# Convolution and max pool: pooled row pairs with a shared middle-row product, seeded by a PSUM to PSUM copy, with GpSimd preparing the input

## The chip, the cores and the metric

One core of one Trainium2 chip. The time is the device time of one execution in microseconds (us), the median over runs; lower is better. The engines are PE (TensorE: matmuls), ACT (ScalarE), DVE (VectorE), POOL (GpSimd) and SP (SyncE, which here only issues DMAs). Each engine works through its own list of instructions in order, and waits at an instruction until the semaphores that it names have come.

## The reference

A 3x3 convolution with zero padding over 16 images of 64 channels and 64x64 pixels, to 128 channels, and then the maximum over 2x2 pixels:

```python
batch, c_in, h, w, c_out, k = 16, 64, 64, 64, 128, 3
x_pad = np.pad(x, ((0, 0), (0, 0), (1, 1), (1, 1)))
conv[b, co] += weight[co, ci, kh, kw] * x_pad[b, ci, kh:kh+h, kw:kw+w]   # over ci, kh, kw
output[b, c, i, j] = np.max(conv[b, c, 2*i:2*i+2, 2*j:2*j+2])
```

All arrays are float32; the matmuls take bf16 operands.

## The kernel before

Two images are worked on at a time: the 64 channels of the first lie on partitions 0 to 63, those of the second on 64 to 127. A matmul with 64 rows of weights uses one half of PE's rows, so a matmul for the one image (L96, into tile pa) and one for the other (L97, into pb) run side by side; the two together are called a pass here. Weights are loaded, each of the nine taps is copied twice beside itself (L52, L53), transposed by PE (L55) and cast to bf16 by ACT (L57), so that each tap's weights lie on both halves of the partitions.

For each pair of images p (8 of them), the float32 rows come in as two pieces of 1 MB (xraw_t and xraw_b, issued on SP's queue), ACT casts the upper half into xpad (L72) and DVE the lower (L73), and POOL clears the two padding rows (L70, L71). Then come 8 chunks c of 8 rows of convolution. For each chunk PE runs nine passes, one a tap, that add up in the PSUM tiles pa and pb; the moving operand is 8 rows of 64 columns of xpad, shifted by the tap (512 columns, or 8x63 = 504 where the tap looks left or right). ACT copies each PSUM tile to SBUF (L107, 512 columns), DVE takes the maximum over neighbouring columns (L109) and then over neighbouring rows (L113) into oacc, which ACT's queue stores in two pieces a pair (L101 and L122, 16 stores in all).

The order of instructions on each engine is set by a scheduler, from the dependences between tiles. The tile pools allow three chunks in PSUM and two pairs of images in SBUF.

Of the kernel before, what the change touches and what calls it, by code (L numbers as in the profile page):

```python
# [1 line left out]

# [5 lines left out]


@with_exitstack
def kernel(
    ctx: ExitStack,
    tc: tile.TileContext,
    x: bass.AP,
    weight: bass.AP,
    pool_size: bass.AP,
    out: bass.AP,
):
    nc = tc.nc  # L20
# [16 lines left out]
    xraw_pool = ctx.enter_context(tc.tile_pool(name="xraw_pool", bufs=2))
    xpad_pool = ctx.enter_context(tc.tile_pool(name="xpad_pool", bufs=2))
    colmax_pool = ctx.enter_context(tc.tile_pool(name="colmax_pool", bufs=8))
    oacc_pool = ctx.enter_context(tc.tile_pool(name="oacc_pool", bufs=2))  # L40

    ident = const.tile([128, 128], FP32)
    make_identity(nc, ident)
# [2 lines left out]
    nc.sync.dma_start(out=wraw, in_=weight.rearrange("a b c d -> a (b c d)"))  # L46

    wk = []
    for k in range(K * K):
        wdup = const.tile([CO, 2, CI], FP32, name=f"wdup_{k}")  # L50
        src = wraw.rearrange("a (ci k) -> a k ci", k=K * K)[:, k, :]
        nc.vector.tensor_copy(out=wdup[:, 0, :], in_=src)  # L52
        nc.vector.tensor_copy(out=wdup[:, 1, :], in_=src)  # L53
        wp = wpsum.tile([128, 128], FP32, name="wpsum")
        nc.tensor.transpose(wp, wdup.rearrange("a b c -> a (b c)"), ident)  # L55
        wt = const.tile([128, CO], BF16, name=f"wt_{k}")
        nc.scalar.copy(out=wt, in_=wp)  # L57
        wk.append(wt)

    out_v = out.rearrange("b c h w -> c b (h w)")  # L60

    for p in range(B // 2):
# [1 line left out]
        xraw_t = xraw_pool.tile([128, H // 2, W], FP32, name="xraw_t")
        xraw_b = xraw_pool.tile([128, H // 2, W], FP32, name="xraw_b")
        nc.sync.dma_start(out=xraw_t, in_=xv[:, 0 : H // 2])
        nc.sync.dma_start(out=xraw_b, in_=xv[:, H // 2 : H])

        xpad = xpad_pool.tile([128, HP, W], BF16)
        nc.gpsimd.memset(xpad[:, 0, :], 0.0)  # L70
        nc.gpsimd.memset(xpad[:, H + 1, :], 0.0)  # L71
        nc.scalar.copy(out=xpad[:, 1 : 33, :], in_=xraw_t)  # L72
        nc.vector.tensor_copy(out=xpad[:, 33 : H + 1, :], in_=xraw_b)  # L73

        oacc = oacc_pool.tile([128, 2, HO * WO], FP32)

        for c in range(NCHUNK):
            y0 = c * ROWS
            pa = psum.tile([128, ROWS, W], FP32, name="pa")
            pb = psum.tile([128, ROWS, W], FP32, name="pb")  # L80
            korder = [1, 4, 0, 3, 6, 2, 5, 8, 7]
            for i, k in enumerate(korder):
                kh, kw = k // K, k % K
                st = i == 0
                sp = i == K * K - 1
                rows = xpad[:, y0 + kh : y0 + kh + ROWS]
                if kw == 1:
                    mv = rows.rearrange("p a b -> p (a b)")
                    oa, ob = pa, pb
                elif kw == 0:  # L90
                    mv = rows[:, :, 0 : W - 1]
                    oa, ob = pa[:, :, 1:W], pb[:, :, 1:W]
                else:
                    mv = rows[:, :, 1:W]
                    oa, ob = pa[:, :, 0 : W - 1], pb[:, :, 0 : W - 1]
                nc.tensor.matmul(oa, wk[k][0:CI, :], mv[0:CI], start=st, stop=sp)  # L96
                nc.tensor.matmul(ob, wk[k][CI:128, :], mv[CI:128], start=st, stop=sp)  # L97

            for half, pt in ((0, pa), (1, pb)):
                if half == 0 and c == 5:  # L100
                    nc.scalar.dma_start(  # L101
                        out=out_v[:, 2 * p : 2 * p + 2, 0 : HO * WO // 2],
                        in_=oacc[:, :, 0 : HO * WO // 2],
                    )
                pv = pt
                sb = colmax_pool.tile([128, ROWS, W], FP32, name=f"sb{half}")
                nc.scalar.copy(out=sb, in_=pv)  # L107
                cm = colmax_pool.tile([128, ROWS, WO], FP32, name=f"cm{half}")
                nc.vector.tensor_tensor(  # L109
                    out=cm, in0=sb[:, :, 0::2], in1=sb[:, :, 1::2],  # L110
                    op=mybir.AluOpType.max,
                )
                nc.vector.tensor_tensor(  # L113
                    out=oacc.rearrange("p b (h w) -> p b h w", h=HO)[
                        :, half, y0 // 2 : y0 // 2 + ROWS // 2, :
                    ],
                    in0=cm[:, 0::2, :],
                    in1=cm[:, 1::2, :],
                    op=mybir.AluOpType.max,
                )  # L120

        nc.scalar.dma_start(  # L122
            out=out_v[:, 2 * p : 2 * p + 2, HO * WO // 2 :],
            in_=oacc[:, :, HO * WO // 2 :],
        )


# [33 lines left out]
```

## Time and profile before

| | |
|---|---|
| median of 3 runs | 146.75 us (146.67 to 147.31) |
| span of the profiled execution, first to last instruction | 145.9 us |
| mean granted TensorE clock over the span | 0.995 |
| PE busy | 131.7 us (90%), 1161 matmuls, 1152 of them tap passes' halves |
| DVE busy | 95.2 us (65%) |
| ACT busy | 86.2 us (59%) |
| POOL busy | 8.6 us (6%) |
| DMA | 25.64 MB, mean 176 GB/s |

The page gives no time of its own for the profiled execution beside its span; the runs' median lies 0.85 us above it. Rows of instruction groups read: line, engine, operation, output tile <- input tiles, shape, count | busy us in total, mean ns of one | us that the engine sat idle ahead of it, and what ended the idle time. Rows of a timeline begin with the start and the duration in us. "PEld" is PE's loading of weights, which overlaps its matmuls.

### The profile page before, as it was taken

The page shows a single profiled execution, that of the slowest core. Times are in us where ns is not written, and L with a number is a line of the kernel's source. Part 1 is how long each engine was busy: PE and PEld are TensorE (multiplying, and loading weights), DVE is VectorE, ACT ScalarE, POOL GpSimd, SP SyncE. Part 2 cuts the span into 40 slices and gives each one's busy share as a digit, 9 for nine tenths or more (in the row PEclk, how much of TensorE's full clock was granted, in tenths as well). Part 3 has the DMA queues.
Part 4 walks back from the last instruction along what each step waited for, and adds up shares of the span by engine and source line. Part 5 has one row for each costly group of instructions (what it writes and reads, how often), then busy time and mean ns, then how long its engine had stood idle before and what let it go on. Part 6 is the DMA issues. An engine that isn't in the chain of part 4 may idle for free.

```text
span 145.9 us, 3022 instructions
## 1 busy us (share of the span) xinstructions
PE 131.7 (90%) x1161; PEld 58.0 (40%) x1161; DVE 95.2 (65%) x282; ACT 86.2 (59%) x146; POOL 8.6 (6%) x22
## 2 busy tenths in 40 slices
PE   0159999999999999999999999999999999999930
PEld 0023344444444444444444444444444444444410
DVE  0630287686768685878679676867686858586770
ACT  3174644578555955597367755695559555463640
POOL 2000000030001200030003000300002000000000
PEclk9999999999999999999999999999999999999997
DMA  5999995308960598139840994030302112030303
GB/s 164 409 427 427 395 332 231 144 2 236 384 247 3 133 344 334 57 63 284 369 152 16 259 408 184 7 146 0 144 4 84 60 67 81 13 131 4 144 0 144
DMA packets 6813, 25.64 MB, mean 176 GB/s; under 512 B 528, under 2 KB 528, under 8 KB 4752
## 3 DMA queue, kind: packets, MB, share of 16 engines
q1 hardware_dynamic: 2448, 17.07, 32.3%
q10 hardware_dynamic: 4352, 8.39, 15.1%
q8 instruction: 9, 0.15, 0.4%
q14 instruction: 4, 0.03, 0.1%
HBM read 17.07 MB, written 8.39 MB: 175 GB/s over the span
## 4 chain that ended last, share of the span: by engine, by line
PE 90%; DMA 4%; ACT 2%; DVE 1%; SPq 0%; issue 0%; ACTq 0%
PE pa L96 86%; DMA xraw_t<-in_x_dram 4%; PE pb L97 2%; PE wpsum L55 2%; ACT xpad L72 1%; DVE cm L109 1%; ACT sb L107 0%; DVE oacc L113 0%; SPq L46 0%; ACT wt L57 0%; ACTq L107 0%
## 5 line engine op out<-in xcount | busy, mean ns | idle before, releaser
L96 PE MATMUL pa<-xpad,wt 64*128 64x504 bf16 (+1 forms) x576 | 127.6, 382 | 0.0
L97 PE MATMUL pb<-xpad,wt 64*128 64x504 bf16 (+1 forms) x576 | 127.6, 382 | 0.0
L96 PEld LDWEIGHTS <-wt 64*128 64x128 bf16 x576 | 54.8, 95 | 70.5 <-issue 3.6
L109 DVE TENSOR_TENSOR cm<-sb 128x256 f32<-128x256 f32 x128 | 53.6, 423 | 35.9 <-ACT sb L107 35.9
L107 ACT COPY sb<-pa 128x512 f32<-128x512 f32 x64 | 37.5, 585 | 46.2 <-PE pb L97 33.0
L97 PEld LDWEIGHTS <-wt 64*128 64x128 bf16 x576 | 54.8, 95 | 0.5 <-issue 0.5
L113 DVE TENSOR_TENSOR oacc<-cm 128x128 f32<-128x128 f32 x128 | 36.8, 292 | 3.9
L107 ACT COPY sb<-pb 128x512 f32<-128x512 f32 x64 | 37.9, 592 | 0.0
L72 ACT CAST xpad<-xraw_t 128x2048 bf16<-128x2048 f32 x8 | 15.3, 1909 | 4.9 <-DMA xraw_t<-in_x_dram 4.9
L70 POOL MEMSET xpad<- 128x64 bf16 x8 | 7.5, 937 | 101.2 <-DVE oacc L113 101.2
L73 DVE CAST xpad<-xraw_b 128x2048 bf16<-128x2048 f32 x8 | 9.8, 1226 | 3.4 <-DMA xraw_b<-in_x_dram 3.4
L55 PE MATMUL wpsum<-ident,wdup 128*128 128x128 f32 x9 | 3.5, 452 | 8.3 <-ACT wt L57 4.2
L71 POOL MEMSET xpad<- 128x64 bf16 x8 | 7.3, 918 | 0.0
L55 PEld LDWEIGHTS wpsum<-ident,wdup 128*128 128x128 f32 x9 | 1.6, 187 | 10.4 <-ACT wt L57 6.2
L52 DVE COPY wdup<-wraw 128x64 f32<-128x64 f32 x9 | 1.9, 209 | 3.7 <-DMA wraw<-in_weight_dram 3.7
L57 ACT CAST wt<-wpsum 128x128 bf16<-128x128 f32 x9 | 2.2, 265 | 3.1 <-PE wpsum L55 3.1
L53 DVE COPY wdup<-wraw 128x64 f32<-128x64 f32 x9 | 1.9, 208 | 0.0
L72 ACT ACT_TABLE_LOAD x1 | 1.3, 1283 | 0.7 <-PEq L142 0.7
masks.py:199 POOL TENSOR_SCALAR_AFFINE_SELECT ident<-ident 128x128 f32<-128x128 f32 x1 | 0.3, 292 | 0.0
masks.py:197 POOL MEMSET ident<- 128x128 f32 x1 | 0.2, 204 | 0.3 <-POOLq L142 0.3
L142 POOL MEMSET const-float32-0.0<- 128x1 f32 x1 | 0.1, 98 | 0.2 <-issue 0.2
L142 POOL MEMSET const-bfloat16-1.0<- 128x1 bf16 x1 | 0.1, 101 | 0.0
(2 smaller groups left out, 0.2 us busy)
## 6 DMA issues: line engine op xcount, KB each, us to landing
xraw_t<-in_x_dram SPq DMA_DIRECT2D x8, 1024.0 KB, 8.5
xraw_b<-in_x_dram SPq DMA_DIRECT2D x8, 1024.0 KB, 7.0
out_dram<-oacc ACTq DMA_DIRECT2D x16, 512.0 KB, 3.1
wraw<-in_weight_dram SPq DMA_DIRECT2D x1, 288.0 KB, 2.9
```

Source lines behind the costliest of these rows:

```text
L52: nc.vector.tensor_copy(out=wdup[:, 0, :], in_=src)
L55: nc.tensor.transpose(wp, wdup.rearrange("a b c -> a (b c)"), ident)
L57: nc.scalar.copy(out=wt, in_=wp)
L70: nc.gpsimd.memset(xpad[:, 0, :], 0.0)
L71: nc.gpsimd.memset(xpad[:, H + 1, :], 0.0)
L72: nc.scalar.copy(out=xpad[:, 1 : 33, :], in_=xraw_t)
L73: nc.vector.tensor_copy(out=xpad[:, 33 : H + 1, :], in_=xraw_b)
L96: nc.tensor.matmul(oa, wk[k][0:CI, :], mv[0:CI], start=st, stop=sp)
L97: nc.tensor.matmul(ob, wk[k][CI:128, :], mv[CI:128], start=st, stop=sp)
L107: nc.scalar.copy(out=sb, in_=pv)
L109: nc.vector.tensor_tensor(out=cm, in0=sb[:, :, 0::2], in1=sb[:, :, 1::2], op=mybir.AluOpType.max,)
L113: nc.vector.tensor_tensor(out=oacc.rearrange("p b (h w) -> p b h w", h=HO)[:, half, y0 // 2 : y0 // 2 + ROWS // 2, :], in0=cm[:, 0::2, :], ...
```

## The change

A pooled row is the maximum of two neighbouring rows of the convolution, an even one y0 and the odd one below it, y1. Write x(a) to x(d) for the four input rows that a pair reads, and w0, w1, w2 for the three rows of taps. Then y0 = w0·x(a) + w1·x(b) + w2·x(c) and y1 = w0·x(b) + w1·x(c) + w2·x(d). The change writes both over a common product with the sum of the middle rows, s = x(b) + x(c): y0 = w1·s + (w2 − w1)·x(c) + w0·x(a), and y1 = w1·s + (w0 − w1)·x(b) + w2·x(d). With three columns of taps that is 3 passes for w1·s, 6 for the rest of y0 and 6 for the rest of y1: 15 passes for 8 row pairs, where two chunks took 18.

A group g is now two images and 8 row pairs (16 rows), 32 groups in all. By function:

- load: float32 rows of a group, 0.5 MB a piece, on SP's queue, eight groups ahead (10 buffers).
- do_s (L152) and do_x (L158), on POOL: the row sums s in bf16 from an add of 128x512, and the cast of the rows to bf16, 128x1024. They are written three groups ahead in the program.
- do_c: 3 passes of w1·s into the PSUM tile y0. seed (L180), on ACT: one copy of 128x1024 from y0 to y1, PSUM to PSUM.
- do_a: the 6 other passes into y0. evac (L187), on ACT: y0 to SBUF, in two copies of 128x512.
- do_b: the 6 other passes into y1, on top of the copied product.
- rowmax (L192), on DVE: the maximum of y1 (PSUM) and the copied y0 (SBUF), 2 x 128x512. finish (L200), on DVE: the maximum over neighbouring columns, 512 results from SBUF. Its store (L203) goes on SP's queue, 0.25 MB a group.

y0 and y1 have two PSUM tiles each, taken in turn. Padding rows are left out rather than cleared: the first and last group of an image pair run three passes with 7 rows for 8. At the start, eight matmuls on zeros run ahead of the weights; the weights are cast and subtracted by DVE, ACT and POOL (L86 to L91), transposed in bf16 by PE in 15 steps (L97) and copied out in two pieces (L105 on DVE, L107 on ACT). The order on every engine is the order of the program, with the automatic scheduling switched off.

```diff
+    ctx.enter_context(tc.manual_schedule())
...
+    for i in range(8):
+        yt = y1[(i // 2) % 2]
+        nc.tensor.matmul(
+            yt[:, i % 2], zeros[:, 0:128], zeros, start=True, stop=True, skip_group_check=True
+        )
...
+    nc.gpsimd.tensor_sub(out=wq[:, 7:10, :], in0=wv[:, 6:9, :], in1=wv[:, 3:6, :])
+    nc.gpsimd.tensor_sub(out=wq[:, 10:13, :], in0=wv[:, 0:3, :], in1=wv[:, 3:6, :])
...
-        nc.gpsimd.memset(xpad[:, 0, :], 0.0)
-        nc.gpsimd.memset(xpad[:, H + 1, :], 0.0)
-        nc.scalar.copy(out=xpad[:, 1 : 33, :], in_=xraw_t)
-        nc.vector.tensor_copy(out=xpad[:, 33 : H + 1, :], in_=xraw_b)
...
+        nc.gpsimd.tensor_add(
+            out=ss[p][:, q * R : (q + 1) * R, :], in0=v[:, 0::2, :], in1=v[:, 1::2, :]
+        )
...
+        nc.gpsimd.tensor_copy(out=xb[p][:, 2 * R * q : 2 * R * (q + 1), :], in_=xf[g])
...
+    def do_a(g):
+        p, q = divmod(g, NQ)
+        taps(y0[g % 2], D2, xrows(p, 2 * q * R + 1))
+        taps(y0[g % 2], G0, xrows(p, 2 * q * R - 1), skip=0 if q == 0 else None)
...
+    def seed(g):
+        nc.scalar.copy(out=y1[g % 2], in_=y0[g % 2])
...
+        nc.scalar.copy(out=ev[g][:, half], in_=y0[g % 2][:, half])
...
+        nc.vector.tensor_tensor(
+            out=rm[g][:, half], in0=y1[g % 2][:, half], in1=ev[g][:, half], op=MAX
+        )
...
+        nc.vector.tensor_tensor(
+            out=o, in0=r[:, :, :, 0::2], in1=r[:, :, :, 1::2], op=MAX
+        )
...
+    for g in range(3):
+        do_s(g)
+        do_x(g)
+    do_c(0)
+    seed(0)
+    for g in range(G):
+        if g + LEAD < G:
+            load(g + LEAD)
+        do_a(g)
+        evac(g, 0)
+        if g + 1 < G:
+            do_c(g + 1)
+            seed(g + 1)
+        do_b(g)
+        evac(g, 1)
+        rowmax(g, 0)
+        rowmax(g, 1)
+        finish(g)
+        if g + 3 < G:
+            do_s(g + 3)
+            do_x(g + 3)
```

The order on the engines, at three places. PE before, at the border of two chunks; a chunk's first matmuls wait until ACT has copied the tiles of three chunks earlier (a matmul and the weights that it takes stand in two rows):

```order
L96 LDWEIGHTS wt_7_137
L96 MATMUL pa_216<-xpad_150,wt_7_137 128x512
L97 LDWEIGHTS wt_7_137
L97 MATMUL pb_217<-xpad_150,wt_7_137 128x512
L96 LDWEIGHTS wt_1_95
L96 MATMUL pa_246<-xpad_150,wt_1_95 128x512 [waits Activation_49]
L97 LDWEIGHTS wt_1_95
L97 MATMUL pb_247<-xpad_150,wt_1_95 128x512 [waits Activation_49]
```

PE after, where B(1), into the second y1 tile, ends and A(2), into the first y0 tile, begins:

```order
L128 LDWEIGHTS wt_125
L128 MATMUL y1_1_84<-xb_143,wt_125 128x8x63
L128 LDWEIGHTS wt_125
L128 MATMUL y0_0_81<-xb_143,wt_125 128x512 [waits Activation_49]
L128 LDWEIGHTS wt_125
L128 MATMUL y0_0_81<-xb_143,wt_125 128x512
```

The wait on ACT now is for the copy seed(2), whose source C(2) was written just ahead of B(1). ACT before, over some chunks of the first pair, has only copies out of PSUM, each waiting for its own chunk:

```order
L72 CAST xpad_402<-xraw_t_398 128x2048 [waits DMAHW3_49]
L107 COPY sb0_176<-pa_156 128x512 [waits PE_49]
L107 COPY sb1_181<-pb_157 128x512 [waits PE_49]
L107 COPY sb0_206<-pa_186 128x512 [waits PE_49]
L107 COPY sb1_211<-pb_187 128x512 [waits PE_49]
L107 COPY sb0_236<-pa_216 128x512 [waits PE_49]
```

ACT after, over groups 1 and 2:

```order
L187 COPY ev_216<-y0_1_82 128x512 [waits PE_49]
L180 COPY y1_0_83<-y0_0_81 128x1024 [waits DVE_49,PE_49]
L187 COPY ev_216<-y0_1_82 128x512
L187 COPY ev_262<-y0_0_81 128x512 [waits PE_49]
L180 COPY y1_1_84<-y0_1_82 128x1024 [waits DVE_49,PE_49]
L187 COPY ev_262<-y0_0_81 128x512
```

The copy from y0 to y1 stands between the two copies of a group, and waits for DVE as well, which must have read the y1 tile two groups earlier. POOL before, at the first pairs of images, has two clearings a pair:

```order
masks.py:199 AFFINE_SELECT ident_76<-ident_76 128x128 [waits Pool_49]
L70 MEMSET xpad_402 128x64
L71 MEMSET xpad_402 128x64
L70 MEMSET xpad_654 128x64 [waits PE_49,DVE_49,Activation_49,Pool_49]
L71 MEMSET xpad_654 128x64
```

POOL after, from the fourth pair of images on, waits for a load at each group, and at each new pair for PE, whose use of the tiles s and xb three pairs earlier must have ended:

```order
L152 TENSOR_TENSOR s_423<-xf_292 128x512 [waits DMAHW7_49]
L158 CAST xb_422<-xf_292 128x1024
L152 TENSOR_TENSOR s_601<-xf_336 128x512 [waits DMAHW1_49,PE_49,Pool_49]
L158 CAST xb_600<-xf_336 128x1024 [waits PE_49,Pool_49]
L152 TENSOR_TENSOR s_601<-xf_380 128x512 [waits DMAHW3_49]
```

What was 16 instructions over the main loop is now 64, two a group.

More of the change, by code (lines that the diff above doesn't have):

```diff
@@ L37 @@
[L37 to L43, printed above, removed]
+    NP = B // 2
+    NQ = 4
+    R = HO // NQ
+    G = NP * NQ
+    LEAD = 8
+    const = ctx.enter_context(tc.tile_pool(name="const", bufs=1))
@@ L45 @@
+    ctx.enter_context(tc.manual_schedule())
+    y0 = [psum.tile([128, 2, R, W], FP32, name=f"y0_{i}") for i in range(2)]
+    y1 = [psum.tile([128, 2, R, W], FP32, name=f"y1_{i}") for i in range(2)]
     wraw = const.tile([CO, CI * K * K], FP32)
     nc.sync.dma_start(out=wraw, in_=weight.rearrange("a b c d -> a (b c d)"))
[L48 to L58, printed above, removed]
@@ L60 @@
-    out_v = out.rearrange("b c h w -> c b (h w)")
-    for p in range(B // 2):
-        xv = x[2 * p : 2 * p + 2].rearrange("b c h w -> (b c) h w")
[L64 to L111, printed above, removed]
-                )
[L113 to L124, printed above, removed]
-        )
@@ new lines, with load @@
+    xb, ss, xf = {}, {}, {}
+    def load(g):
+        p, q = divmod(g, NQ)
+        xv = x[2 * p : 2 * p + 2].rearrange("b c h w -> (b c) h w")
+        xf[g] = xf_pool.tile([128, 2 * R, W], FP32, name="xf")
+        nc.sync.dma_start(out=xf[g], in_=xv[:, 2 * R * q : 2 * R * (q + 1), :])
+    for g in range(LEAD):
+        load(g)
+    zeros = const.tile([128, 512], BF16)
+    nc.vector.memset(zeros, 0.0)
+    ident = const.tile([128, 128], BF16)
+    make_identity(nc, ident)
+    for i in range(8):
[3 more added lines that the diff above has]
+        )
@@ new lines @@
+    wv = wraw.rearrange("a (ci k) -> a k ci", k=K * K)
+    wq = const.tile([CO, 16, CI], BF16)
+    nc.vector.tensor_copy(out=wq[:, 1:4, :], in_=wv[:, 3:6, :])
+    nc.vector.tensor_copy(out=wq[:, 4:7, :], in_=wv[:, 0:3, :])
+    nc.scalar.copy(out=wq[:, 0, :], in_=wv[:, 8, :])
+    nc.scalar.copy(out=wq[:, 13:16, :], in_=wv[:, 6:9, :])
+    nc.gpsimd.tensor_sub(out=wq[:, 7:10, :], in0=wv[:, 6:9, :], in1=wv[:, 3:6, :])
+    nc.gpsimd.tensor_sub(out=wq[:, 10:13, :], in0=wv[:, 0:3, :], in1=wv[:, 3:6, :])
@@ new lines @@
+    wt = const.tile([128, 15, CO], BF16)
+    for h, (lo, hi) in enumerate(((0, 8), (8, 15))):
+        tp = y0[1][:, h].rearrange("p a b -> p (a b)").bitcast(BF16)
+        for j in range(lo, hi):
+            nc.tensor.transpose(
+                tp[:, (j - lo) * 128 : (j - lo + 1) * 128],
+                wq[:, j : j + 2, :].rearrange("a b c -> a (b c)"),
+                ident,
+            )
+        src = tp[:, 0 : (hi - lo) * 128]
+        dst = wt[:, lo:hi, :].rearrange("p a b -> p (a b)")
+        if h == 0:
+            nc.vector.tensor_copy(out=dst, in_=src)
+        else:
+            nc.scalar.copy(out=dst, in_=src)
@@ new lines, in wtop, with wbot, taps @@
+    def wtop(m):
+        return wt[0:CI, (m + 1) % 15, :]
+    def wbot(m):
+        return wt[CI:128, m, :]
+    G1, G0, D2, D0, G2 = 0, 3, 6, 9, 12
+    def taps(dst, m0, rows, start=False, skip=None):
+        for kw in (1, 0, 2):
+            i0, i1 = 0, R
+            if skip == 0:
+                i0 = 1
+            if skip == R - 1:
+                i1 = R - 1
+            o0, o1, c0, c1 = (0, W, 0, W) if kw == 1 else (1, W, 0, W - 1) if kw == 0 else (0, W - 1, 1, W)
+            for half, wsel in ((0, wtop), (1, wbot)):
+                lo = half * CI
+                nc.tensor.matmul(
+                    dst[:, half, i0:i1, o0:o1],
+                    wsel(m0 + kw),
+                    rows(lo, i0, i1, c0, c1),
+                    start=start and kw == 1,
+                    stop=True,
+                    skip_group_check=True,
+                )
@@ new lines, in xrows, with get, do_s @@
+    def xrows(p, first):
+        v = xb[p]
+        def get(lo, i0, i1, c0, c1):
+            a = first + 2 * i0
+            return v[lo : lo + CI, a : first + 2 * (i1 - 1) + 1 : 2, c0:c1]
+        return get
+    def do_s(g):
+        p, q = divmod(g, NQ)
+        if q == 0:
+            xb[p] = xb_pool.tile([128, H, W], BF16, name="xb")
+            ss[p] = s_pool.tile([128, HO, W], BF16, name="s")
+        v = xf[g]
+        nc.gpsimd.tensor_add(
+            out=ss[p][:, q * R : (q + 1) * R, :], in0=v[:, 0::2, :], in1=v[:, 1::2, :]
+        )
@@ new lines, in do_b, with evac, rowmax @@
+    def do_b(g):
+        p, q = divmod(g, NQ)
+        taps(y1[g % 2], D0, xrows(p, 2 * q * R))
+        taps(y1[g % 2], G2, xrows(p, 2 * q * R + 2), skip=R - 1 if q == NQ - 1 else None)
+    def seed(g):
+        nc.scalar.copy(out=y1[g % 2], in_=y0[g % 2])
+    ev, rm = {}, {}
+    def evac(g, half):
+        if half == 0:
+            ev[g] = ev_pool.tile([128, 2, R, W], FP32, name="ev")
+        nc.scalar.copy(out=ev[g][:, half], in_=y0[g % 2][:, half])
+    def rowmax(g, half):
+        if half == 0:
+            rm[g] = rm_pool.tile([128, 2, R, W], FP32, name="rm")
+        nc.vector.tensor_tensor(
+            out=rm[g][:, half], in0=y1[g % 2][:, half], in1=ev[g][:, half], op=MAX
+        )
@@ new lines, in finish @@
+    def finish(g):
+        p, q = divmod(g, NQ)
+        o = o_pool.tile([128, 2, R, WO], FP32, name="o")
+        r = rm[g]
+        nc.vector.tensor_tensor(
+            out=o, in0=r[:, :, :, 0::2], in1=r[:, :, :, 1::2], op=MAX
+        )
+        nc.sync.dma_start(
+            out=out[2 * p : 2 * p + 2, :, q * R : (q + 1) * R, :].rearrange(
+                "b c h w -> c b (h w)"
+            ),
+            in_=o.rearrange("p b h w -> p b (h w)"),
+        )
+        del rm[g], ev[g]
+    for g in range(3):
+        do_s(g)
+        do_x(g)
```

26 lines of the change are left out of this document (19 added, 7 removed).

## The prediction

> **What bounds the kernel now.** I read the engine totals first, then the chain of work that ended last, then the groups of instructions by form, then the timeline at the two ends and at the places that the change touches. The totals and the chain's shares by line:
>
> ```profile
> PE 131.7 (90%) x1161; PEld 58.0 (40%) x1161; DVE 95.2 (65%) x282; ACT 86.2 (59%) x146; POOL 8.6 (6%) x22
> ...
> PE pa L96 86%; DMA xraw_t<-in_x_dram 4%; PE pb L97 2%; PE wpsum L55 2%; ACT xpad L72 1%; DVE cm L109 1%; ACT sb L107 0%; DVE oacc L113 0%; SPq L46 0%; ACT wt L57 0%; ACTq L107 0%
> ```
>
> PE is 90% busy and nearly the whole chain is its tap passes; a pass is one L96 and one L97 matmul that run side by side on the two halves of the rows. Nothing but fewer or faster passes, a shorter start or a shorter tail can help. The groups (mean ns of one after the comma):
>
> ```profile
> L96 PE MATMUL pa<-xpad,wt 64*128 64x504 bf16 x384 | 94.9, 381 | 0.0
> L109 DVE TENSOR_TENSOR cm<-sb 128x256 f32<-128x256 f32 x128 | 53.6, 423 | 35.9 <-ACT sb L107 35.9
> L96 PE MATMUL pa<-xpad,wt 64*128 64x512 bf16 x192 | 53.2, 383 | 0.0
> L107 ACT COPY sb<-pb 128x512 f32<-128x512 f32 x64 | 37.9, 592 | 0.0
> L113 DVE TENSOR_TENSOR oacc<-cm 128x128 f32<-128x128 f32 x128 | 36.8, 292 | 3.9
> L72 ACT CAST xpad<-xraw_t 128x2048 bf16<-128x2048 f32 x8 | 15.3, 1909 | 4.9 <-DMA xraw_t<-in_x_dram 4.9
> L55 PE MATMUL wpsum<-ident,wdup 128*128 128x128 f32 x9 | 3.5, 452 | 8.3 <-ACT wt L57 4.2
> L52 DVE COPY wdup<-wraw 128x64 f32<-128x64 f32 x9 | 1.9, 209 | 3.7 <-DMA wraw<-in_weight_dram 3.7
> ```
>
> A matmul's own duration (381 ns) overlaps its successor, so the price of a pass is read from start to start, at the end of the run:
>
> ```profile
> 137.69 0.38 PE L96 MATMUL pa<-xpad,wt 64*128 64x512 bf16 x1
> ...
> 137.90 0.38 PE L96 MATMUL pa<-xpad,wt 64*128 64x512 bf16 x1
> ...
> 138.15 0.58 ACT L107 COPY sb<-pa 128x512 f32<-128x512 f32 x1 [0.87 <-PE pb L97]
> ...
> 138.63 0.59 ACT L107 COPY sb<-pb 128x512 f32<-128x512 f32 x1
> ...
> 139.63 0.38 PE L96 MATMUL pa<-xpad,wt 64*128 64x512 bf16 x1
> 140.10 0.58 ACT L107 COPY sb<-pa 128x512 f32<-128x512 f32 x1 [0.87 <-PE pb L97]
> ...
> 140.72 0.43 DVE L109 TENSOR_TENSOR cm<-sb 128x256 f32<-128x256 f32 x1 [0.53 <-ACT sb L107]
> 141.18 0.29 DVE L113 TENSOR_TENSOR oacc<-cm 128x128 f32<-128x128 f32 x1
> ...
> 142.16 0.38 ACTq L122 DMA_DIRECT2D out_dram<-oacc  x1
> ```
>
> 137.69 and 139.63 are the last passes of two neighbouring chunks: nine passes in 1.94 us, 0.2156 us each. The pass of 137.69 gives way at 137.90 and ScalarE starts on its result at 138.15: 0.25 us from PE to ScalarE. The start:
>
> ```profile
> 3.68 0.22 DVE L52 COPY wdup<-wraw 128x64 f32<-128x64 f32 x1 [3.68 <-DMA wraw<-in_weight_dram]
> ...
> 6.89 1.90 ACT L72 CAST xpad<-xraw_t 128x2048 bf16<-128x2048 f32 x1 [4.88 <-DMA xraw_t<-in_x_dram]
> ...
> 9.37 1.23 DVE L73 CAST xpad<-xraw_b 128x2048 bf16<-128x2048 f32 x1 [3.35 <-DMA xraw_b<-in_x_dram]
> ...
> 11.82 0.27 ACT L57 CAST wt<-wpsum 128x128 bf16<-128x128 f32 x1 [0.68 <-PE wpsum L55]
> 12.25 0.18 PEld L55 LDWEIGHTS wpsum<-ident,wdup 128*128 128x128 f32 x1 [0.44 <-ACT wt L57]
> ...
> 13.60 0.60 PE L96 MATMUL pa<-xpad,wt 64*128 64x504 bf16 x1
> ...
> 14.00 0.63 PE L96 MATMUL pa<-xpad,wt 64*128 64x504 bf16 x1
> ...
> 14.43 0.63 PE L96 MATMUL pa<-xpad,wt 64*128 64x504 bf16 x1
> ```
>
> Weights land at 3.68, 1 MB of images at 6.89, the next at 9.37 (so 0.5 MB takes 1.24 us). Weights then ping-pong between PE and ScalarE; three passes are done by 13.60, when the unbroken run begins. Its first passes are 0.43 us apart; in the chain the pace turns between these rows:
>
> ```profile
> 18.05 0.29 PE pa L96
> 18.55 0.21 PE pa L96
> ```
>
> From ScalarE back to PE: 11.82 + 0.27 = 12.09, and PE resumes at 12.25, 0.16 us.
>
> **The change, part by part.** The sum is made on the span, 145.9 us; the median of the runs shown is 146.75, so 0.85 us lie around the span and stay.
>
> *Passes.* 32 groups (two images, 16 rows) with 15 passes each, 480 for 576: 96 × 0.2156 = 20.7 us less. The eight first groups leave out one row of eight in three passes: 3 passes, 0.65 us less (the eight last groups' saving falls where PE waits for ScalarE anyway, see below). Twelve of the 15 read every second row; the 64x504 form, broken into rows as well, costs 381 ns against 383, so I add nothing; bound: a tenth of 384 passes, 8 us.
>
> *The PSUM to PSUM copy.* PE runs A(g), 6 passes; C(g+1), 3; B(g), 6; A(g+1). A(g+1) adds into the bank that seed(g+1) copies from, so it waits for it. Between C's end and A(g+1) lie B's six passes, 1.29 us. The seed has 1024 columns: 0.59 + 512 × (1.909 − 0.59)/1536 = 1.03 us. Bounds: twice the start-to-start of the L107 copies (138.15 to 138.63), 0.96; twice their duration, 1.18. With the two hand-overs the wait takes 0.25 + 1.03 + 0.16 = 1.44 us, 0.15 more than B covers. Times 31: +4.5 us (+2.5 to +9.2; nothing, if writes to PSUM are much shorter: no row shows one from ScalarE). Ahead of the seed, evac(g,0) starts 0.25 after A and takes 0.59, and C lasts 0.65: it is out of the way. ScalarE's load is 2 × 0.59 + 1.03 = 2.21 us of a group's 3.38 (3.23 of passes and the wait).
>
> *VectorE.* Two maxima of 512 columns with one side in PSUM, and one of 512 from SBUF. By L113 and L109, (0.423 − 0.292)/128 = 1.02 ns a column: 0.69 us each, 2.06 a group. From PSUM no row shows it; below, the 0.59 of ScalarE's copy, above, twice 0.69. Even 1.38 × 2 + 0.69 = 3.45 only touches the group's 3.38. seed(g+2) needs both maxima of g; they end 0.25 + 1.4 us after B(g), and that seed starts a whole A and C (1.94) plus 0.15 after it: hidden, by 0.4.
>
> *GpSimd.* It had 8.6 us of work; now each group needs an add of 512 columns and a cast of 1024. Its rows, with VectorE's beside the two odd ones:
>
> ```profile
> 0.27 0.10 POOL L142 MEMSET const-float32-1.0<- 128x1 f32 x1
> ...
> 0.73 0.20 POOL masks.py:197 MEMSET ident<- 128x128 f32 x1 [0.29 <-POOLq L142]
> ...
> 0.87 0.15 POOL L70 MEMSET xpad<- 128x64 bf16 x1
> ...
> 1.13 0.29 POOL masks.py:199 TENSOR_SCALAR_AFFINE_SELECT ident<-ident 128x128 f32<-128x128 f32 x1
> ...
> 31.34 1.20 POOL L70 MEMSET xpad<- 128x64 bf16 x1 [29.74 <-DVE oacc L113]
> 31.42 1.17 POOL L71 MEMSET xpad<- 128x64 bf16 x1
> ...
> 31.22 1.23 DVE L73 CAST xpad<-xraw_b 128x2048 bf16<-128x2048 f32 x1
> ```
>
> A memset's slope is (0.20 − 0.10)/127 = 0.8 ns a column, the select's (it reads, compares, writes) 1.5. Cast: 0.10 + 1024 × 0.8 = 0.92 to 1.64; it compares nothing, so I take 1.1. Add: one stream at 0.8, 0.51, to two reads at 1.5, 1.64; I take 1.2. Sum 2.3 us a group (1.43 to 3.28). The 0.15 us memset took 1.20 us while VectorE's cast ran and ended with it (32.54 against 32.45): the two shut each other out. If the SBUF maximum does that once a group, GpSimd needs 2.3 + 0.69 = 2.99 of 3.38, still hidden; the margin is 0.39 us.
>
> The Trainium skill, "GPSIMD Engine Reference", section 3.1, measures 4497 ns for a two-input add of 2048 columns, by which (an estimate) the add is about 1.1 us; its section 4.1 calls one-input work roughly line-rate but elementwise work the wrong use of this engine. With those the sum would stay as it is, and no run here shows either figure yet.
>
> *Loads and stores.* Loads go in 32 pieces of 0.5 MB (1.24 us each of 3.38); stores move from ScalarE's queue to SP's, where load(g+9) stands behind the store of g, which waits for VectorE. That load is used eight groups later (27 us), so it hides.
>
> *Start.* GpSimd's two subtractions and the other engines' casts end by 4.9 us; 15 transposes at about 0.1 (bounds 0.05 and the 0.45 of L55's fp32 ones) in two lots with VectorE's copy of 1024 columns (0.16 + 1.04) and ScalarE's 896 (0.92) between give wt by 8.6; the row sum has its 0.5 MB at 5.65 and is ready at 6.9. C(0) at 7.4 takes 1.28 at the slow pace, seed(0) ends near 10.0 and the unbroken run starts at 10.1, again with three passes done: 3.5 us less than 13.60 (4.6 less to 2.0 more). The slow pace of the first eleven passes I leave as it was; if the eight zero matmuls end it, 2.3 us less.
>
> *Tail.* From the last pass's end (139.84) to the store's issue (142.16) it was 2.32; now 0.25 + 3 × 0.69 + 0.05. The last store carries half the bytes: 0.5 us less (up to 1.4 more by the PSUM bound).
>
> Sum: 145.9 − 20.7 − 0.65 + 4.5 − 3.5 − 0.5 = 125.05, and 0.85 around it: **125.9 us**.
>
> **The rivals.** (1) *The seed hides*: if it takes under 0.88 us, PE never waits, 125.9 − 4.5 = 121.4. For it: only 0.15 us decides. Against: the nearest rows give 0.96 at the least. The Trainium skill, "ScalarE: Activation LUTs", section "Step-by-step: what each stage is for", says ScalarE is closer to PSUM and writes there sooner; no run here shows by how much.
>
> (2) *GpSimd becomes the bound.* Its first add starts at 5.65; then 32 groups of p; then B(30), A(31), B(31), 3.9; tail 5.5 and 0.85: 15.9 + 32p. It decides from p = 3.38 on. With the select's rate for the cast, 1.64 + 1.2 + 0.69 = 3.53, 128.9; with both upper ends 3.28 + 0.69 = 3.97, 142.9. A middle one, 3.7, 134.3. For it: the select is the only row that reads, and it is slow. Against: a cast needs less per column.
>
> (3) *Slower: every maximum shuts GpSimd out*, not only the one with both inputs in SBUF; the other two also read one input there. Then p = 2.3 + 3 × 0.69 = 4.37 and the time 155.7. It ends over the old time from p = 4.09. For it: the memset pair above, against one-input work. Against: that cast ran at 0.6 ns a column, faster than any maximum, so it may hold more of the path than they do. The Trainium skill, "SBUF — State Buffer", section "Who interferes with whom", has it that VectorE blocks GpSimd's reads with two SBUF inputs or in its faster two-port modes, not with one; by that rule only L200's maximum counts, as in the sum.
>
> (4) *The passes don't get cheaper*: reading every second row would have to cost 0.054 us a pass (20.9/384) to eat the gain. The two equal forms speak against it.
>
> **How the numbers follow.** Forecast 0.57 (122.5 to 131 by its own bounds), rival 1 0.10, rival 2 0.22, rival 3 0.09, rival 4 0.02. The range 119 to 141 leaves out rival 3, rival 4 and the top of rival 2 (p over 3.91, 0.05), and 0.01 below. Half a per cent is about what can be told from no change here. Faster: 0.57 + 0.10 + 0.22 less 0.02 for p near or over 4.09 = 0.87; within: 0.02; slower: 0.11.
>
> **What the profile after would show.** PE at 480 passes, 0.2156 apart within A, C and B; before each A a gap of about 0.15 us that ScalarE's L180 ends, L180 near 1.03 us; L152 plus L158 near 2.3 us of GpSimd and GpSimd ahead of PE by several groups; L192 and L200 near 0.69; PE's unbroken run from about 10 us. The prediction is wrong if PE's waits end on GpSimd's L152 or L158 in the middle of the run, or if L180's gap is above 0.3 or absent.

## The result and the profile after

The changed kernel takes 120.19 us in the median of five runs (118.44 to 121.77) against 147.17 before: 0.810 of the time, 95% interval 0.804 to 0.816. On another chip it took 119.18 (118.14 to 120.30 in six runs), 0.808 (0.805 to 0.812). A run over 1.5% above the fastest of its kernel counts as slow: it is in the medians and ranges given here but not in the intervals, and where too few others are left no interval is given. The forecast was 125.9 in a range of 119 to 141: the direction and the sum's largest term held, the time came out 5.7 us lower, near the lower end of the range. The profiled execution took 120.19, its span is 118.4. Totals, and the chain's shares by line, of the page after:

```profile
PE 109.7 (93%) x983; PEld 49.9 (42%) x983; DVE 74.8 (63%) x100; ACT 69.7 (59%) x100; POOL 81.8 (69%) x72
...
PE y L128 88%; DMA xf<-in_x_dram 4%; POOL s L152 1%; ACT y L180 1%; DVE rm L192 1%; DVE o L200 1%; SPq L59 0%; DVEq L192 0%
```

PE is still the bound and the chain is its tap passes. GpSimd has gone from 6% to 69% without getting into the chain, but for its first row sum. The chain in order of time (start, us, what):

```profile
5.95 1.27 POOL s L152
...
7.27 0.84 PE y L128 x6
...
8.13 1.01 ACT y L180
...
9.18 103.93 PE y L128 x944
...
114.53 0.69 DVE o L200
```

C(0) waits for the first row sum, A(0) for the first seed, and from 9.18 us on the chain runs through PE alone for 103.93 us. In all of the middle no seed, no row sum and no cast stands in it. The groups that answer to those shown before:

```profile
L192 DVE TENSOR_TENSOR rm<-y,ev 128x512 f32<-128x512 f32 x64 | 41.2, 686 | 34.9 <-PE y L128 33.3
L187 ACT COPY ev<-y 128x512 f32<-128x512 f32 x64 | 37.6, 589 | 37.3 <-PE y L128 37.3
L152 POOL TENSOR_TENSOR s<-xf 128x512 bf16<-128x512 f32 x32 | 45.0, 1408 | 11.3 <-DMA xf<-in_x_dram 9.9
L158 POOL CAST xb<-xf 128x1024 bf16<-128x1024 f32 x32 | 36.8, 1150 | 0.0
L180 ACT COPY y<-y 128x1024 f32<-128x1024 f32 x32 | 31.9, 997 | 1.0 <-PE y L128 0.7
L200 DVE TENSOR_TENSOR o<-rm 128x512 f32<-128x512 f32 x32 | 31.7, 989 | 1.1
```

Two groups in the middle of the run, from the timeline (PE's rows are merged by operand; 6 matmuls are 3 passes), and, last, a row of the list of waits (engine, line waited for: us in total, times, longest us):

```profile
60.28 0.81 PE L128 MATMUL y<-s,wt 64*128 64x512 bf16 x6
...
60.93 2.65 PE L128 MATMUL y<-xb,wt 64*128 64x512 bf16 x24
...
61.13 1.00 ACT L180 COPY y<-y 128x1024 f32<-128x1024 f32 x1
...
62.18 5.00 PEld L128 LDWEIGHTS <-wt 64*128 64x128 bf16 x50 [0.32 <-ACT y L180]
62.35 1.03 POOL L158 CAST xb<-xf 128x1024 bf16<-128x1024 f32 x1
62.42 1.29 DVE L192 TENSOR_TENSOR rm<-y,ev 128x512 f32<-128x512 f32 x2 [1.15 <-PE y L128]
63.41 0.81 PE L128 MATMUL y<-s,wt 64*128 64x512 bf16 x6
63.42 1.27 POOL L152 TENSOR_TENSOR s<-xf 128x512 bf16<-128x512 f32 x1
...
63.75 1.49 DVE L200 TENSOR_TENSOR o<-rm 128x512 f32<-128x512 f32 x1
64.06 2.76 PE L128 MATMUL y<-xb,wt 64*128 64x512 bf16 x24
64.27 1.00 ACT L180 COPY y<-y 128x1024 f32<-128x1024 f32 x1
64.64 1.50 POOL L158 CAST xb<-xf 128x1024 bf16<-128x1024 f32 x1
...
66.66 0.81 PE L128 MATMUL y<-s,wt 64*128 64x512 bf16 x6
...
PEld L128 <- ACT y L180: 3.8, 8, 1.6
```

In the second group C ends at 64.06, the seed runs from 64.27 to 65.27, and B's six passes (1.29) last until 65.35: A begins then, and PE doesn't wait. The first group is a border of two image pairs, where three passes of B leave out a row and B takes 1.21 (1.29 less 3/8 of a pass): it is over at 62.14, the seed at 62.13, and A's weights load at 62.18, with the seed as what they waited for. PE stands for some 0.04 us there. The row of waits has eight such cases, the first seed and the seven borders; in the other 24 groups the seed is hidden, by some 0.04 us. The rows of 63.42 to 64.64 show VectorE and GpSimd holding each other up: L200 begins in the middle of L152 and takes 1.49 us for its usual 0.69, and L158, next to start, takes 1.50 for its usual 1.03. The L158 of 62.35, beside which L192 alone runs, takes its 1.03.

### The profile page after: what moved, and what is told of

It reads as the page before. It is cut to its first block, busy times and chain, and to the rows that moved or that the text cites. A ratio compares the mean times of both kernels' runs of the same rounds, so it can differ in the third digit from the quotient of the medians.

```text
span 118.4 us, 2534 instructions
## 1 busy us (share of the span) xinstructions
PE 109.7 (93%) x983; PEld 49.9 (42%) x983; DVE 74.8 (63%) x100; ACT 69.7 (59%) x100; POOL 81.8 (69%) x72
## 4 chain that ended last, share of the span: by engine, by line
PE 88%; DMA 4%; DVE 1%; POOL 1%; ACT 1%; issue 1%; SPq 0%; DVEq 0%
PE y L128 88%; DMA xf<-in_x_dram 4%; POOL s L152 1%; ACT y L180 1%; DVE rm L192 1%; DVE o L200 1%; SPq L59 0%; DVEq L192 0%
## 5 line engine op out<-in xcount | busy, mean ns | idle before, releaser
L128 PE MATMUL y<-xb,wt 64*128 64x504 bf16 (+3 forms) x768 | 88.5, 377 | 1.1 <-ACT y L180 1.1
L128 PEld LDWEIGHTS <-wt 64*128 64x128 bf16 x960 | 47.5, 95 | 58.4 <-ACT y L180 3.8
L192 DVE TENSOR_TENSOR rm<-y,ev 128x512 f32<-128x512 f32 x64 | 41.2, 686 | 34.9 <-PE y L128 33.3
L187 ACT COPY ev<-y 128x512 f32<-128x512 f32 x64 | 37.6, 589 | 37.3 <-PE y L128 37.3
L152 POOL TENSOR_TENSOR s<-xf 128x512 bf16<-128x512 f32 x32 | 45.0, 1408 | 11.3 <-DMA xf<-in_x_dram 9.9
L158 POOL CAST xb<-xf 128x1024 bf16<-128x1024 f32 x32 | 36.8, 1150 | 0.0
L180 ACT COPY y<-y 128x1024 f32<-128x1024 f32 x32 | 31.9, 997 | 1.0 <-PE y L128 0.7
L200 DVE TENSOR_TENSOR o<-rm 128x512 f32<-128x512 f32 x32 | 31.7, 989 | 1.1
L128 PE MATMUL y<-s,wt 64*128 64x504 bf16 (+1 forms) x192 | 26.4, 382 | 0.3 <-POOL s L152 0.3
L80 PE MATMUL y<-zeros 128*128 128x512 bf16 x8 | 3.6, 630 | 1.2 <-DVE zeros L74 1.2
L107 ACT COPY wt<-y 128x896 bf16<-128x896 bf16 x1 | 0.9, 905 | 2.5 <-PE y L97 2.5
L97 PE MATMUL y<-ident,wq 128*128 128x128 bf16 x15 | 1.6, 269 | 0.8 <-DVE wt L105 0.8
L86 DVE CAST wq<-wraw 128x192 bf16<-128x192 f32 x1 | 0.5, 498 | 2.6 <-DMA wraw<-in_weight_dram 2.6
L97 PEld LDWEIGHTS <-wq 128*128 128x128 bf16 x15 | 1.4, 126 | 1.5 <-issue 0.9
L105 DVE COPY wt<-y 128x1024 bf16<-128x1024 bf16 x1 | 0.7, 692 | 1.0 <-PE y L97 1.0
L91 POOL TENSOR_TENSOR wq<-wraw 128x192 bf16<-128x192 f32 x1 | 0.8, 793 | 0.0
```

What stands on the lines that cost most here:

```text
L80: nc.tensor.matmul(yt[:, i % 2], zeros[:, 0:128], zeros, start=True, stop=True, skip_group_check=True)
L97: nc.tensor.transpose(tp[:, (j - lo) * 128 : (j - lo + 1) * 128], wq[:, j : j + 2, :].rearrange("a b c -> a (b c)"), ident,)
L107: nc.scalar.copy(out=dst, in_=src)
L128: nc.tensor.matmul(dst[:, half, i0:i1, o0:o1], wsel(m0 + kw), rows(lo, i0, i1, c0, c1), start=start and kw == 1, stop=True, skip_group_che ...
L152: nc.gpsimd.tensor_add(out=ss[p][:, q * R : (q + 1) * R, :], in0=v[:, 0::2, :], in1=v[:, 1::2, :])
L158: nc.gpsimd.tensor_copy(out=xb[p][:, 2 * R * q : 2 * R * (q + 1), :], in_=xf[g])
```

## The experiments

**What the shared product is worth: 18 passes.** No row sum, no seed; C takes w1·x(b), A takes w2·x(c) in place of the difference's product, and B begins with w1·x(c):

```diff
-        nc.gpsimd.tensor_add(
-            out=ss[p][:, q * R : (q + 1) * R, :], in0=v[:, 0::2, :], in1=v[:, 1::2, :]
-        )
...
-            lambda lo, i0, i1, c0, c1: st[lo : lo + CI, q * R + i0 : q * R + i1, c0:c1],
+            xrows(p, 2 * q * R),
...
-        taps(y0[g % 2], D2, xrows(p, 2 * q * R + 1))
+        taps(y0[g % 2], G2, xrows(p, 2 * q * R + 1))
...
-        taps(y1[g % 2], D0, xrows(p, 2 * q * R))
+        taps(y1[g % 2], G1, xrows(p, 2 * q * R + 1), start=True)
+        taps(y1[g % 2], G0, xrows(p, 2 * q * R))
...
-        nc.scalar.copy(out=y1[g % 2], in_=y0[g % 2])
```

> The pair isn't shared here: 18 passes a group as in the kernel before, no row sum on GpSimd, no seed copy; the start, the loads, the casts on GpSimd and the tail are as in the changed kernel. Theory (the time went with the passes): PE stays the bound, 96 passes of 0.2156 us come back, 120.2 + 20.7 = 141 us, with GpSimd at about 1.0 us a group. Rival (the gain comes from the start, the casts taken off ScalarE and VectorE and the finer groups): the time stays within 3 us of 120.

138.11 us (137.97 to 139.65), 0.944 of before (0.938 to 0.950). Its chain has one piece of PE:

```profile
7.32 124.90 PE y L128 x1152
```

It begins at 7.32, for there is no first row sum or seed to wait for, and holds 576 passes of 0.217 us. The theory holds: of the whole change's 27.7 us (146.91 to 119.18 on the one chip), this kernel brings 8.4 without the sharing (146.49 to 138.11 on the other), which leaves 19.3 for it. The 96 passes are 20.7; the wait for the first row sum and seed gives about 1.0 of them back (8.96 with three passes done, in the chain of the changed kernel's second run, against 7.32 with none). The 8.4 us lie between two kernels with the same number of passes: 5.9 of them are the unbroken run's earlier start (13.60 with two passes done to 7.32 with none) and 1.3 the rows left out at the borders, both worked out and not taken apart by a run.

**How far the seed hides: its place.** Both copies of y0 go ahead of the next seed in ScalarE's order.

```diff
         evac(g, 0)
+        evac(g, 1)
         if g + 1 < G:
             do_c(g + 1)
             seed(g + 1)
         do_b(g)
-        evac(g, 1)
```

> Only ScalarE's order is changed: both copies of y0 to SBUF go ahead of the next group's seed, which so starts about 1.16 us after A ends and not 0.85. Theory (the seed is hidden, but by less than 0.1 us: in the trace it ends 62.13 and A begins 62.22): PE now waits some 0.27 us before each A, L180 is what ends these waits, and the time is 120.2 + 31 x 0.27 = 128.6 us. Rival (the seed has slack, its wait was priced too high because ScalarE to PE or the copy itself is much shorter): no change, 120.

130.62 us in the median of four runs (128.15 to 130.92), where 128.6 was expected. From the timeline:

```profile
51.43 0.83 PE L128 MATMUL y<-s,wt 64*128 64x512 bf16 x6
51.65 1.07 ACT L187 COPY ev<-y 128x512 f32<-128x512 f32 x2 [1.56 <-PE y L128]
52.08 1.40 PE L128 MATMUL y<-xb,wt 64*128 64x512 bf16 x12
52.61 1.03 ACT L180 COPY y<-y 128x1024 f32<-128x1024 f32 x1
53.70 1.39 PE L128 MATMUL y<-xb,wt 64*128 64x512 bf16 x12 [0.22 <-ACT y L180]
...
54.92 0.81 PE L128 MATMUL y<-s,wt 64*128 64x512 bf16 x6
```

The seed starts 0.53 us behind C's end (52.08) in place of 0.20, ends at 53.64, and A starts 0.06 later. B's passes were over at 53.37: PE stood for 0.33 us, which over 31 groups makes 10.2. The theory holds, and the rows give the price of the way back to PE, 0.06.

**How far the seed hides: its length.** On the kernel with ten more filling matmuls (below), the seed is issued as two copies.

```diff
-        nc.scalar.copy(out=y1[g % 2], in_=y0[g % 2])
+        for half in range(2):
+            nc.scalar.copy(out=y1[g % 2][:, half], in_=y0[g % 2][:, half])
```

> The kernel with the ten filling matmuls (118.4 to 119.3), with the seed as two copies of 512 columns for one of 1024. By the rows of such copies that takes 0.48 + 0.59 = 1.07 us for 0.997. Theory (from PE to ScalarE 0.20, the seed 0.997 and back 0.06 make 1.26 of B's 1.29 us: a margin of 0.03 to 0.09): the longer seed makes PE wait 0.00 to 0.04 us a group, 0 to 1.3 us more, and L180's rows show up as what ends PE's idle time. Rival (the margin is larger, 0.1 us or more): no wait anywhere, 119.0.

123.80 us (123.51 to 124.41), 0.841 of before (0.838 to 0.845): 4.7 us more than with one copy (119.09, on another chip), where 0 to 1.3 was expected.

```profile
61.24 0.83 PE L137 MATMUL y<-s,wt 64*128 64x512 bf16 x6
...
61.89 2.84 PE L137 MATMUL y<-xb,wt 64*128 64x512 bf16 x24
62.11 1.17 ACT L190 COPY y<-y 128x512 f32<-128x512 f32 x2
...
64.56 0.81 PE L137 MATMUL y<-s,wt 64*128 64x512 bf16 x6
```

The two copies take 1.17 us together and not 1.07: two of L187's in a row, which go to SBUF, overlap (1.07 for 2 × 0.59 in the rows of the last run), these two don't. 0.22 + 1.17 + 0.06 is 1.45 us, 0.16 over B's 1.29, and 31 × 0.16 = 5.0. So the miss is the copy's price; the mechanism is the expected one, and it shows how thin the cover is: 0.20 + 0.997 + 0.06 = 1.26 of 1.29.

**More cover for the seed.** C moves between A's two halves (do_a keeps the passes of w2 − w1, do_a2 takes those of w0), and the seed ahead of both copies of y0.

```diff
         taps(y0[g % 2], D2, xrows(p, 2 * q * R + 1))
+
+    def do_a2(g):
+        p, q = divmod(g, NQ)
         taps(y0[g % 2], G0, xrows(p, 2 * q * R - 1), skip=0 if q == 0 else None)
...
         do_a(g)
-        evac(g, 0)
         if g + 1 < G:
             do_c(g + 1)
             seed(g + 1)
+        do_a2(g)
+        evac(g, 0)
+        evac(g, 1)
         do_b(g)
-        evac(g, 1)
```

> PE runs A's first three passes, C of the next group, A's last three passes, B; ScalarE runs the seed and then both copies of y0. The seed now has nine passes (1.94 us) to hide behind and not six (1.29). Theory (the seed is hidden by 0.05 to 0.1 us, so that some executions wait at it and others don't): the trace with no wait gains nothing, but the spread of 118.4 to 121.8 shrinks towards its lower end, median 118 to 119. Rival (the seed has slack and the spread comes from the start): median and spread as in the unedited kernel.

120.53 us (118.39 to 121.71 in six runs), 0.811 (0.806 to 0.816), beside the unedited kernel on the same chip:

> The changed kernel itself, unedited, beside the next three on one chip. Both theories: 118.4 to 122 us as in its first five runs; what is looked for is the spread, and how the span stands to the granted clock.

119.18 (118.14 to 120.30). Neither the median nor the spread shrinks, so the theory on the spread falls: thin as the seed's cover is, it isn't what parts a run of 118.4 from one of 120 or 121. The rival, the start, stays.

**Keeping PE busy ahead of the unbroken run.** awake(n, ys) issues n more matmuls on zeros into the tiles ys.

```diff
         if h == 0:
             nc.vector.tensor_copy(out=dst, in_=src)
+            awake(4, y1)
         else:
             nc.scalar.copy(out=dst, in_=src)
+            awake(2, y1)
...
     do_c(0)
+    awake(4, [y1[1]])
     seed(0)
```

> Ten more matmuls on zeros keep PE busy between the transposes' two lots, behind them, and behind C(0) while ScalarE copies the first seed. The first nine passes behind the first seed took 3.45 us where 1.94 would do, with a granted clock of 0.50 to 0.59. Theory (the idle stretches ahead of them bring the slow pace): the slow stretch goes, 1.5 us less, 118.7. Rival (the pace comes back only after so much time in any case, or the filling matmuls delay C(0)): the same time, or up to 1 us more.

119.09 us (118.44 to 119.27 in five runs), 0.810 (0.808 to 0.813). The same stretch, 9.10 to 11.50 us, in the run of the unedited kernel and in this one (columns: length, PE busy and count, PEld, DVE, ACT, POOL, granted clock, DMA share, GB/s):

```profile
9.10:11.50 2.40, 2.40 (x14) 0.92 (x12) 0.00 (x0) 0.00 (x0) 2.40 (x3) 0.50 1.00 346
...
9.10:11.50 2.40, 2.40 (x26) 1.10 (x24) 0.00 (x0) 1.05 (x2) 2.40 (x4) 1.00 0.97 336
```

Fourteen matmuls against 26, at a granted clock of 0.50 against 1.00. From the chains, the unbroken runs begin alike:

```profile
8.96 103.79 PE y L128 x954
...
8.95 102.35 PE y L137 x954
```

1.44 us less, as expected for this execution. The median didn't move (119.09 for 119.18). The spans suggest why: the unedited kernel's six are 116.4 to 116.8 us three times and 118.0 to 118.5 three times, so that probably only some of its executions have the slow stretch, and the five with the filling matmuls, 116.6 to 117.4, have it in none. Only the profiled executions show the pace itself. The Trainium skill, "TensorE: Matmul & The Clock Gate", Part 1, has PE throttled to half rate by default, with recent activity releasing it. This case's two rows agree, with 0.50 behind idle stretches and 1.00 behind the filling matmuls; but the profile's clock needn't show the pace (last section).

**Both.** The two edits together.

> The two edits together. If both hold, 117 us (1.5 us less for the start, and the spread at its lower end); if only the seed's order counts, 118 to 119; if only the start, 118.7 with the unedited kernel's spread.

118.60 us (118.45 to 119.15 in five runs), 0.808 (0.806 to 0.811). As narrow as with the filling matmuls alone, and no faster than the unedited kernel by anything that the intervals can tell. The filling matmuls have a price too: in this profiled execution the slow stretch is gone, but they stand in the chain ahead of C(0), which begins at 7.90 us in this chain and at 7.04 in that of the filling matmuls alone.

**Fewer matmuls on zeros ahead of the weights.** The changed kernel without the ten of the last runs; its own loop runs four times for eight.

```diff
-    for i in range(8):
+    for i in range(4):
```

> The changed kernel with four matmuls on zeros at the start for eight (one for each PSUM bank of y1, which the accumulation on copied data needs). Theory (PE's idle time ahead of the unbroken run sets how many passes run at the slow pace): PE stands idle from about 3 us to 4.6 us, more passes are slow, as in the kernel before (eleven or more at 0.43), and the time is 119.5 to 122, hardly ever 118.4. Rival (what counts is only the gap behind the first seed): as the changed kernel, 118.1 to 121.8 with some of the runs at 118.4.

121.21 us (120.69 to 122.02), 0.824 (0.820 to 0.827), with no run near 118.4. From its chain:

```profile
7.08 1.48 PE y L128 x6
...
9.63 103.98 PE y L128 x954
```

C(0) takes 1.48 us and not 0.84, so the seed and A(0) come 0.67 later than in the second run of the unedited kernel, and the slow pace goes on through A(0) and C(1). This one execution doesn't settle it, since C(0) is as slow (1.44 us) in the profiled execution of the kernel with C between A's halves, which has all eight. The runs speak for the theory: none of these six is under 120.69, and five of the unedited kernel's eleven are under 119. Keeping PE busy at the start is worth some 2 us in the median, on two chips.

**GpSimd as the bound.** A second cast of the same rows, into a tile that nothing reads.

```diff
         nc.gpsimd.tensor_copy(out=xb[p][:, 2 * R * q : 2 * R * (q + 1), :], in_=xf[g])
+        nc.gpsimd.tensor_copy(out=scr, in_=xf[g])
```

> GpSimd casts each group's rows twice, the second time into a tile that nothing reads. Theory (VectorE's maximum from SBUF and GpSimd's instructions shut each other out, which adds 0.25 to 0.45 us to GpSimd's group): GpSimd becomes the bound at 1.27 + 2 x 1.03 + 0.25 to 0.45 = 3.6 to 3.8 us a group, 17 + 32p = 132 to 138 us. Rival (the stretched rows of the trace are not lost time for GpSimd): p = 3.33, only just over PE's 3.24, 123.5 us.

131.65 us (131.56 to 131.88), 0.898 (0.894 to 0.902). The chain's shares by line, and GpSimd's and VectorE's groups:

```profile
POOL scr L160 28%; POOL s L153 26%; POOL xb L159 25%; PE y L129 4%; DMA xf<-in_x_dram 4%; DVE o L202 2%; DMA out_dram<-o 2%; DVE rm L194 1%; ACT y L182 1%; ACT ev L189 0%; SPq L59 0%; DVEq L194 0%
...
L160 POOL CAST scr<-xf 128x1024 bf16<-128x1024 f32 x32 | 42.0, 1312 | 0.0
L153 POOL TENSOR_TENSOR s<-xf 128x512 bf16<-128x512 f32 x32 | 41.4, 1294 | 0.9 <-DMA xf<-in_x_dram 0.9
...
L202 DVE TENSOR_TENSOR o<-rm 128x512 f32<-128x512 f32 x32 | 39.7, 1242 | 1.1
```

The chain is GpSimd's now. Its row sums begin from 6.1 to 118.6 us (the rows below), which is 112.5/31 = 3.63 us a group, within the 3.6 to 3.8 expected; the time came out just under the 132 to 138.

**What GpSimd shares with VectorE.** The same, with VectorE's maximum over neighbouring columns as a reduction with one input.

```diff
-        nc.vector.tensor_tensor(
-            out=o, in0=r[:, :, :, 0::2], in1=r[:, :, :, 1::2], op=MAX
+        nc.vector.tensor_reduce(
+            out=o.rearrange("p b h w -> p (b h w)"),
+            in_=r.rearrange("p b h (w t) -> p (b h w) t", t=2),
+            op=MAX,
+            axis=mybir.AxisListType.X,
         )
```

> As the run with two casts, but VectorE's maximum over neighbouring columns is a reduction with one input of 1024 columns in place of a maximum with two SBUF inputs of 512. Theory (two SBUF inputs are what shuts GpSimd out): no GpSimd instruction is stretched any more, p = 3.33 and the time 123.5 us, 9 or more below the run with the maximum; the reduction takes about 1.15 us and is hidden. Rival (any VectorE work on SBUF costs GpSimd): GpSimd's rows are stretched as much as with the maximum, and the time is the same as there or longer.

121.71 us (121.49 to 122.04), 0.830 (0.826 to 0.834): 9.9 us less, though the reduction itself takes longer (1.22 us, the last row below, for the maximum's 0.69 when nothing holds it up). Least, median and largest duration of GpSimd's three lines, in the two runs:

```profile
L153 POOL TENSOR_TENSOR s<-xf x32: 1261/1267/1708, 6.1 to 118.6; 128x512 bf16<-128x512 f32 x32
L159 POOL CAST xb<-xf x32: 1026/1034/1517, 7.3 to 119.8; 128x1024 bf16<-128x1024 f32 x32
L160 POOL CAST scr<-xf x32: 1033/1498/1511, 8.3 to 120.8; 128x1024 bf16<-128x1024 f32 x32
...
L153 POOL TENSOR_TENSOR s<-xf x32: 1257/1265/1283, 6.0 to 105.0; 128x512 bf16<-128x512 f32 x32
L159 POOL CAST xb<-xf x32: 1026/1027/1049, 7.2 to 106.3; 128x1024 bf16<-128x1024 f32 x32
L160 POOL CAST scr<-xf x32: 1030/1032/1053, 8.2 to 107.2; 128x1024 bf16<-128x1024 f32 x32
...
L202 DVE TENSOR_REDUCE o<-rm 128x512 f32<-128x1024 f32 x32 | 39.0, 1220 | 1.1
```

With two SBUF inputs on VectorE, GpSimd's casts stretch to 1.5 us; with one, nothing stretches, and PE is the bound again, though GpSimd works 87% of the span. The Trainium skill, "SBUF — State Buffer", section "Who interferes with whom", has a VectorE instruction with two SBUF inputs contend with a GpSimd instruction that reads SBUF, and a reduction never. The trace agrees: 1.50 us for the casts beside the one, 1.05 at most beside the other.

**The casts on VectorE.** On the kernel with the filling matmuls:

```diff
-        nc.gpsimd.tensor_copy(out=xb[p][:, 2 * R * q : 2 * R * (q + 1), :], in_=xf[g])
+        nc.vector.tensor_copy(out=xb[p][:, 2 * R * q : 2 * R * (q + 1), :], in_=xf[g])
```

> The kernel with the filling matmuls, with the cast of the rows (L158) on VectorE and only the row sums on GpSimd. VectorE then has 2 x 0.69 + 0.69 + about 0.65 us a group, 2.7 of 3.24, and GpSimd 1.27. Theory (GpSimd's part of the change is a choice of place, the passes carry the gain): PE stays the bound, 118.5 to 120.5, with GpSimd's sum and VectorE's cast and SBUF maximum stretched where they meet. Rival (only with the casts on GpSimd does VectorE keep up): VectorE falls behind by what the shared path costs it, at 3.4 us a group or more, 124 or more.

122.17 us (120.64 to 123.32 in six runs), 0.827 (0.822 to 0.832): 3.1 us more than with GpSimd's casts (119.09, on another chip), between the two forecasts.

```profile
PE y L137 55%; DVE rm L201 13%; DVE o L209 9%; DVE xb L167 3%; ACT y L189 3%; PE y L80 3%; PE y L86 2%; PE y L104 1%; DVE zeros L74 0%; DVEq L209 0%; DVEq L201 0%; ACTq L189 0%
...
L161 POOL TENSOR_TENSOR s<-xf 128x512 bf16<-128x512 f32 x32 | 45.0, 1414 | 44.6 <-DMA xf<-in_x_dram 42.6 <-PE y L137 1.9
...
L167 DVE CAST xb<-xf 128x1024 bf16<-128x1024 f32 x32 | 32.1, 1008 | 0.0
...
L209 DVE TENSOR_TENSOR o<-rm 128x512 f32<-128x512 f32 x32 | 29.9, 935 | 1.1
```

VectorE is busy for 101.2 us, 3.2 a group, and its maxima and the seeds behind them appear in the chain. So casting on GpSimd is worth some 3 us here, about a sixth of what the sharing brings.

## Why the prediction was right, and which step of it failed

- *Passes.* Right: 480 passes; a group of 15 takes 3.24 us from C to C (63.41 to 66.66 in the timeline), 0.216 a pass. Reading every second row costs nothing (rival 4 falls). The left-out rows were mis-sized by little: at the border of two image pairs, where B and the next A are both short, a group takes 3.13 us (21.71 to 24.84), 0.11 less than 3.24 and not 0.08; with the first A and the last B some 0.9 us over the run for 0.65.
- *The seed.* This is the step that failed: "+4.5 us", a wait of 0.15 us before each A. In 24 of the 31 groups there is no wait, and at the seven borders it is some 0.04; rival 1, with a chance of 0.10, is what happened. By the prediction's own sign, L180's gap absent, this part of it was wrong. All three pieces were a little long: PE to ScalarE 0.20 (put at 0.25), the copy 0.997 (1.03), the way back 0.06 (0.16). Together 1.26 us for 1.44, on the other side of B's 1.29. Rival 1's own bound, a copy under 0.88, was off for the same reason, since it rested on the two hand-overs: by the measured ones it is 1.03. A sum that decides at 0.15 us should not have stood at 0.57 to 0.10.
- *GpSimd.* Right: 2.3 us a group was forecast, and by the unstretched rows it is 1.27 + 1.03 = 2.30. The agreement is partly luck: the add was put at 1.2 and the cast at 1.1, within wide bounds. What VectorE adds was put too high: 0.69 a group, measured (45.0 + 36.8)/32 − 2.30 = 0.26. Rival 2 stays a rival; two casts for one made it true, at 131.65. By its own formula it passes the forecast at p = 3.44 (15.9 + 32 × 3.44 = 126.0), not at 3.38.
- *All maxima shut GpSimd out* (rival 3). Wrong: L192, with one SBUF input, takes 680 to 694 ns in every one of its 64 rows, with GpSimd busy beside it for most of the run, and GpSimd's rows are not longer beside it (the L158 of 62.35 above, and every GpSimd row of the run with the reduction). Only L200 collides.
- *VectorE.* 0.69 was forecast for the three maxima; L192, with one side in PSUM, takes 686 ns.
- *Start.* Forecast at 10.1, came at 9.18: 0.7 of the difference is that C(0) and the hand-over to the seed took 0.86 us (7.27 to 8.13) and not the 1.53 of the slow pace. The prediction also miscounted the passes ahead of 13.60: the timeline before has two matmuls of L96 (9.62, 11.72) and two of L97 (10.78, 12.66) there, two passes and not three, which makes 0.2 us more. The slow pace holds A(0) and C(1), 3.45 us (9.18 to 12.63) for nine passes that take 1.94 elsewhere: 1.5 us lost, where the 2.2 of before (eleven passes from 13.60 to 18.18) was left in the sum.
- *Tail.* 5.3 us from the last matmul's end (113.1) to the end of the span, for 5.9 before (139.63 + 0.38 = 140.0); 0.5 had been taken off, 0.6 came.
- *Around the span.* Put at 0.85, measured 120.19 − 118.4 = 1.8: the span shown of before probably belongs to an execution slower than the median (on the next chips the kernel before has 144.7 beside 146.5).

With the terms as measured: 125.05 − 4.5 (seed) − 0.3 (rows left out, the waits at the borders among them) − 1.1 (start) − 0.7 (slow pace) − 0.1 (tail) = 118.35 against a span of 118.4, and 1.8 around it. That the time lies in the range owes something to luck: the 1.0 us too little around the span made up for part of what the seed was too much, and five of the eleven runs of the changed kernel, 118.14 to 118.56, lie under the range.

## What to carry to other kernels

Fewer passes on the engine that bounds pay almost in full (19.3 of 20.7 us here) as long as what replaces them fits between two uses of the same PSUM tile: write down the hand-overs and the copy, see what PE does meanwhile, and if the two sums differ by a tenth of a microsecond, carry both outcomes. GpSimd can take one-input and two-input work on the input side, at 1.0 ns a column for a cast and 2.5 for an add here, if VectorE's instructions with two SBUF inputs are few. At the start keep PE busy: four of the eight matmuls on zeros ahead of the weights are worth some 2 us here, while ten more narrow the spread (118.44 to 119.27 for 118.14 to 120.30) and leave the median where it was.
